# A two-layer hybrid decoder step: the first token rows transposed inside the gate stage instead of ahead of it

## The chip, the cores and the metric

The kernel runs on one core of a Trainium2 chip. A core has five engines, each with its own instruction stream: TensorE (PE in the profile, its weight loads apart as PEld) for matrix products, VectorE (DVE), ScalarE (ACT), GpSimd (POOL) and SyncE (SP), which here only issues loads and stores. ACT and POOL issue loads too. PE writes to PSUM, here five banks for this stage; the other engines take results from there to SBUF, the working memory. The metric is the device time of one execution in microseconds; three runs of the kernel before gave 2650.81, 2652.7 and 2654.59.

## The reference

One inference step over 1,048 token rows of width 1,024: 16 learned meta rows, 1,024 prompt rows, and 8 sample rows that have their own states. Everything is in float32. Layer 0 mixes tokens with a Conformer convolution module, layer 1 with an RWKV-7 recurrence; a squared-ReLU MLP with a hidden width of 4,096 follows each. Only the beginning matters here:

```
def _rmsnorm(x, g):
    y = x * rsqrt(mean(x * x, -1) + RMS_EPS)
    return y * g

hn = _rmsnorm(h, norm_mix[0])
u = hn @ w_pw1 + b_pw1                      # 1024 -> 2048
u = u[..., :D] * sigmoid(u[..., D:])        # the gate
c = depthwise causal convolution of u, 31 taps, + b_dw
out = silu(layernorm(c)) @ w_pw2 + b_pw2
h = h + out
h = h + relu(rmsnorm(h) @ w_in)**2 @ w_out
```

The weights are stored by rows of channels; the vectors (`norm_mix`, `b_pw1` and so on) are small.

## The kernel before, in words

Layer 0 keeps activations with channels on the 128 partitions and tokens along the row, so the 1,024 channels are 8 blocks (`KT`), and the tokens are cut in three groups of 352, 348 and 348 (`G0`). A product in near-float32 precision is made of three (`mm3`, L188): weights and activations are each split into a high part in a shorter format and the low remainder, and high x high, low x high and high x low are added in PSUM. `dense` (L197) does that over the 8 channel blocks, 24 PE products for one block of output channels. The weights' high part is cast by ACT (L158), the low part made by POOL in four pieces (L165); raw weights come by loads on SP into a pool of five buffers tagged "raw".

The input comes with tokens on the partitions. `transpose_x` (L475) turns a group round, in these steps:

1. For group 0, `stage_vecs` (L454) clears a tile on POOL and loads the first small vectors into its rows, every other one by ACT's queue and by POOL's.
2. `load_x` (L436) loads the group's rows in three tiles on SP; for each, ACT squares it with a row sum (L444), takes the root (L445), and DVE the reciprocal (L446).
3. For each channel block, PE transposes the three tiles with the identity into a bank, `tx` (L483), and DVE (group 0) or ACT (group 1) copies it to `h` (L485), which is needed only for the residual add after the convolution module. Group 2 goes through memory.
4. For group 0, `place_vecs` (L462) transposes the staged vectors and copies them to `pvec`, from which all per-channel scales and biases are read.
5. `between` starts the first weight block; then DVE builds `dg`, the identity scaled by each row's reciprocal root (L496).
6. For each channel block, PE multiplies the tiles by `dg`, which transposes and normalizes in one product, `tn` (L500); ACT scales it by `norm_mix` into the high part `hn_h` (L502), DVE makes the low part `hn_l` (L503).

Group 0 goes through all of this before its gate stage. Then `load_dw` (L467) brings in and transposes the 31 depthwise tap weights (`ptw`, L472). The gate stage is `pw1` (L511): for each of 8 blocks of output channels two `dense` calls, `ps_g` and `ps_a`, a sigmoid on ACT and a combining step on DVE (L521).

The instructions carry priorities in program order, and a planner, which simulates a timeline, fixes each engine's order: where an engine would be idle in that timeline, work from later in the program is brought forward. Two things are by hand. Group 0's `transpose_x` runs under `manual_schedule` for ACT (L701), so that ACT's order there is as written. And the work for the next group is mixed into the gate stage by `filler` (L303): `pw1` calls a function 32 times, in the middle of and behind each `dense`, and each call advances a generator so that its units (each `yield` tells how many) are spread evenly over the 32 calls. For group 1 that is `transpose_x(1)` with 4 units for the loads and 8 + 8 for its blocks.

The x tiles come from a pool of three buffers (`xin`), so group 1's loads wait until group 0's tiles have been read for the last time. The convolution of group 0 (L539, L542) runs on DVE from the moment that its inputs and the tap weights are there.

Of the kernel before, what the change touches and what calls it, by code (L numbers as in the profile page):

```python
# [8 lines left out]
F32 = mybir.dt.float32  # L9
# [7 lines left out]
P = 128  # L17
D = 1024
KT = D // P
# [27 lines left out]
def hybrid_step(tc, x_prompt, x_sample, state_conv, state_shift, state_wkv, meta_tokens,  # L47
# [8 lines left out]
    nc = tc.nc  # L56
    ctx = ExitStack()
    with ctx:
# [4 lines left out]
        ident = consts.tile([P, P], F32, name="ident")  # L63
# [9 lines left out]
        d_x2 = dram.tile([P, KT, G0[2][1]], F32, name="d_x2")  # L73
# [32 lines left out]
        col, nrow = {}, 0  # L106
        for name, ap in vecs:
            n = ap.shape[0]
# [85 lines left out]
        def bank(name, tag="mm"):  # L194
            return cur[tag].tile([P, 512], F32, name=name, tag=tag)
# [20 lines left out]
        def tt(name, tag):  # L216
            return cur["tmp"].tile([P, cur["n"]], F32, name=name, tag=tag)
# [178 lines left out]
        with ExitStack() as l0:  # L396
# [16 lines left out]
            h = {}  # L413
# [36 lines left out]
            def load_vecs(tiles):  # L450
                for i in tiles:
                    place_vecs(i, stage_vecs(i))

            def stage_vecs(i):  # L454
                st = cur["raw"].tile([P, D], F32, name=f"stg{i}", tag="raw")[:, :P]
                nc.gpsimd.memset(st, 0.0)
                for q, (name, ap) in enumerate(v for v in vecs if col[v[0]] // P == i):
                    r = col[name] % P
                    (nc.gpsimd if q % 2 else nc.scalar).dma_start(st[r:r + ap.shape[0], :], ap)
                return st  # L460

            def place_vecs(i, st):  # L462
                pt = bank("ptp")
                nc.tensor.transpose(pt[:, :P], st, ident)
                nc.vector.tensor_copy(pvec[:, i * P:(i + 1) * P], pt[:, :P])

            def load_dw():  # L467
                wst = cur["raw"].tile([P, D], F32, name="wst", tag="raw")[:CW, :]
                nc.scalar.dma_start(wst, conv_w_dw.rearrange("l w c -> (l w) c"))
                pt = bank("ptw")  # L470
                for k in range(KT):
                    nc.tensor.transpose(pt[:, k * CW:(k + 1) * CW], wst[:, k * P:(k + 1) * P], ident[:CW, :CW])  # L472
                nc.vector.tensor_copy(wdw, pt[:, :KT * CW].rearrange("p (k w) -> p k w", k=KT))

            def transpose_x(g, ah, al, between=lambda: None):  # L475
                n = G0[g][1]
                staged = stage_vecs(0) if g == 0 else None
                tiles = load_x(xin, g)
                yield 4
                for k in range(KT):  # L480
                    ps = bank(f"tx{g}_{k}")
                    for c, w, xt, ss in tiles:
                        nc.tensor.transpose(ps[:, c:c + w], xt[:w, k * P:(k + 1) * P], ident[:w, :w])  # L483
                    if g < 2:
                        (nc.scalar.copy if g else nc.vector.tensor_copy)(h[g][:, k, :n], ps[:, :n])  # L485
                    else:
                        t = tt(f"xs{k}", "t1")
                        nc.scalar.copy(t[:, :n], ps[:, :n])
                        nc.sync.dma_start(d_x2[:, k, :], t[:, :n])
                    yield 1  # L490
                if g == 0:
                    place_vecs(0, staged)
                between()
                dg = stat(f"dg{g}", "acc0", 1)
                for c, w, xt, ss in tiles:
                    nc.vector.tensor_scalar(dg[:w, c:c + w], ident[:w, :w], ss[:w, 2:3], None, op0=ALU.mult)  # L496
                for k in range(KT):
                    ps = bank(f"tn{g}_{k}")
                    for c, w, xt, ss in tiles:
                        nc.tensor.matmul(ps[:, c:c + w], xt[:w, k * P:(k + 1) * P], dg[:w, c:c + w], start=True, stop=True)  # L500
                    gk = vec("norm_mix", k)
                    nc.scalar.activation(ah[:, k, :n], ps[:, :n], AF.Copy, scale=gk)  # L502
                    nc.vector.scalar_tensor_tensor(al[:, k, :n], ps[:, :n], gk, ah[:, k, :n].bitcast(F32),  # L503
                                                   op0=ALU.mult, op1=ALU.subtract)
                    yield 1

            def pw1_weights(g, m):
                yield load_col(conv_w_pw1[0], KT + m, f"pg{g}_{m}", nc.gpsimd)
                yield load_col(conv_w_pw1[0], m, f"pa{g}_{m}", nc.gpsimd)
# [181 lines left out]
            with ExitStack() as s:  # L691
                TX = 32
                EARLY = 1
                xin = pool(s, "xin", 3)
                fill, rest = filler(8 * KT, ([ranked(CV0, conv(0)), ranked(CV0, ln_silu(0))], EARLY * (15 * KT // 2 + 2 + 2 * MW + KT)))
                for g in range(2):
                    h[g] = residp[(g + 1) % 2].tile([P, KT, N0], F32, name=f"h0_{g}", tag="h")
                acts = [new_act(actp[(g + 1) % 2], f"hn{g}", N0) for g in range(2)]
                ready = []
                first = pw1_weights(0, 0)  # L700
                with tc.manual_schedule(engines={nc.scalar.engine}):  # L701
                    for _ in transpose_x(0, *acts[0], lambda: ready.append(next(first))):
                        pass
                    ready.append(next(first))
                load_dw()
                for g in range(3):
                    nxt, tail = iter(()), ()
                    if g < 2:
                        if g:
                            acts.append(new_act(actp[1], "hn2", N0))  # L710
                        nxt, tail = filler(TX, ([transpose_x(g + 1, *acts[g + 1])], 4 + 2 * KT))

                    def both():
                        if g:
                            fill()
                        if g < 2:
                            nxt()
                    pw1(g, acts[g], both, [] if g else ready)
                    for _ in tail:
                        pass  # L720
                    if g == 0:
                        load_vecs(range(1, ntile))

                zt = xin.tile([P, D], F32, name="zt", tag="xt")[:, :KT * HS].rearrange("p (k t) -> p k t", k=KT)
                nc.gpsimd.memset(zt, 0.0)
                for q in range(4):
                    nc.scalar.dma_start(d_ab[0].rearrange("p k i (j t) -> p k (i j) t", j=2)[:, :, q, :], zt)
                nc.scalar.dma_start(d_v[META:HS, 0:KT * HS], zt[:HS - META].rearrange("p k t -> p (k t)"))
                nc.scalar.dma_start(d_v[META:HS, KT * HS:], zt[:HS - META].rearrange("p k t -> p (k t)"))

                own, prev = (xin.tile([P, D], F32, name=f"lr{s_}", tag="xt").rearrange("p (k c) -> p k c", k=KT) for s_ in "op")
                for cs, j, src in ((HALF[0], 1, rwkv_w1[0]), (HALF[1], 4, rwkv_a1[0])):
                    nc.sync.dma_start(own[:, :, cs], src.rearrange("(k p) c -> p k c", p=P))
                    for k in range(KT):
                        nc.scalar.activation(prev[:, k, cs], own[:, k, cs], AF.Copy, scale=vec("x_mix", j * KT + k))
                for k in range(0, KT, 2):
                    nc.gpsimd.tensor_sub(own[:, k:k + 2], own[:, k:k + 2], prev[:, k:k + 2])
                for s_, t in enumerate((own, prev)):
                    nc.sync.dma_start(d_lr[:, :, s_], t)
# [15 lines left out]
        for i, op in enumerate((ALU.is_gt, ALU.is_ge)):  # L755
            v = m_ar[:HS, i * HS:(i + 1) * HS]
# [448 lines left out]
        st = {"done": -1, "inv": -1, "credit": 0.0, "decoded": False, "free": 0, "normed": -1}  # L1205
# [582 lines left out]
```

## Time and profile before

The execution that was profiled took 2651.75 us; the others are listed above.

| | |
|---|---|
| median of three runs | 2652.7 us |
| profiled execution, whole | 2651.75 us |
| its span, first to last instruction | 2649.8 us |
| PE busy | 2594.1 us, 98% |
| DVE, ACT, POOL busy | 1717.6, 1128.8, 1456.7 us |
| first row transpose on PE | 5.42 us |
| first scaled product (`tn`) | 12.06 us |
| first gate product (`ps_g`) | 20.34 us |
| end of group 0's gate stage on PE | 90 us |

All times within the execution are microseconds from the start of the span. In lists of instructions each line gives start, duration, engine, line of the kernel, operation, tiles, and in brackets how long the engine was idle before and what released it. "q" behind an engine's name is its queue of loads. In the chain of the work that ended last, each line gives start and duration of a piece, followed back from the end at each step to what released it. A product of full float32 operands shows as two records, a transpose as one.

### The profile page before, as it was taken

Reading aid. Unit: us, or ns where it says so; the run is one execution under the profiler, and the core shown is the slowest. Engines: PE = TensorE matmul, PEld = TensorE weight load, DVE = VectorE, ACT = ScalarE, POOL = GpSimd, SP = SyncE. Lnnn points to the kernel's source line nnn. Section 1 sums busy time; section 2 is a strip of 40 time slices with the busy share of each in tenths; the row PEclk is TensorE's granted clock in tenths of the full one; section 3 lists DMA queues with packets and bytes.
Section 4 is the critical chain, followed back from the end, with each engine's and each line's share of the span. In section 5 each row is a group of like instructions: output and inputs, shape, how many; then the busy total and the mean of one; then the engine's idle time right before and its main releaser. Section 6 shows DMA issues by size and latency. Waiting matters only on the chain.

```text
span 2649.8 us, 51719 instructions
## 1 busy us (share of the span) xinstructions
PE 2594.1 (98%) x19956; PEld 2432.9 (92%) x19956; DVE 1717.6 (65%) x3610; ACT 1128.8 (43%) x2093; POOL 1456.7 (55%) x2060
## 2 busy tenths in 40 slices
PE   9999999999999999999999999899999999999998
PEld 8999999999999999777777777789999999999998
DVE  6999999997444444445757567686679554444435
ACT  5546435444444333243344545545444542222223
POOL 7677878878878777022211113476588763333331
PEclk9999999999999999999999999999999999999999
DMA  7663544554446543677776867898575542222211
GB/s 190 172 168 108 167 141 133 160 172 137 138 138 187 155 136 112 191 211 202 214 184 181 213 160 194 218 207 195 142 219 174 153 132 65 72 68 69 72 48 44
DMA packets 602060, 400.24 MB, mean 151 GB/s; under 512 B 96128, under 2 KB 548928, under 8 KB 601814
## 3 DMA queue, kind: packets, MB, share of 16 engines
q1 hardware_dynamic: 573764, 360.08, 49.6%
q0 software_dynamic: 8720, 26.35, 3.0%
q10 hardware_dynamic: 19330, 10.49, 1.4%
q8 instruction: 158, 2.59, 0.4%
q14 instruction: 88, 0.72, 0.1%
HBM read 338.94 MB, written 58.83 MB: 150 GB/s over the span
## 4 chain that ended last, share of the span: by engine, by line
PE 85%; DVE 8%; ACT 2%; issue 2%; DMA 1%; POOL 1%; SPq 0%; ACTq 0%; DVEq 0%; POOLq 0%
PE ps_in L190 8%; PE ps_in L192 8%; PE ps_in L191 8%; PE out L190 8%; PE out L191 8%; PE out L192 8%; PE pk L922 4%; PE pr L922 4%; PE pv L922 3%; PE ps_g L190 1%; PE ps_o L192 1%; PE ps_g L191 1%; PE ps_g L192 1%; PE ps_oo L190 1%; PE ps_o L190 1%
## 5 line engine op out<-in xcount | busy, mean ns | idle before, releaser
L165 POOL TENSOR_TENSOR wo_lo<-wo_raw,wo_hi 128x256 fp32r<-128x256 f32 x736 | 543.0, 770 | 286.6 <-ACT wo_hi L158 279.2
L165 POOL TENSOR_TENSOR wi_lo<-wi_raw,wi_hi 128x256 fp32r<-128x256 f32 x640 | 474.5, 774 | 238.3 <-ACT wi_hi L158 237.9
L190 PE MATMUL out<-hh,wo_hi 128*128 128x352 f32 (+2 forms) x1536 | 497.5, 324 | 8.1 <-DVE h L360 6.5
L360 DVE TENSOR_TENSOR h<-h,out 128x352 f32<-128x352 f32 (+2 forms) x768 | 386.9, 512 | 168.2 <-PE out L192 166.6
L190 PE MATMUL ps_in<-m_h,wi_hi 128*128 128x352 f32 (+2 forms) x1536 | 494.0, 322 | 0.0
L192 PE MATMUL ps_in<-m_l,wi_hi 128*128 128x352 f32 (+2 forms) x1536 | 492.8, 321 | 0.7 <-DVE m_l L288 0.7
L191 PE MATMUL out<-hh,wo_lo 128*128 128x352 f32 (+2 forms) x1536 | 492.5, 321 | 0.0
L191 PE MATMUL ps_in<-m_h,wi_lo 128*128 128x352 f32 (+2 forms) x1536 | 491.5, 320 | 0.0
L192 PE MATMUL out<-hl,wo_hi 128*128 128x352 f32 (+2 forms) x1536 | 490.8, 320 | 0.0
L542 DVE SCALAR_TENSOR_TENSOR cv<-u,wdw,cv 128x348 f32<-128x348 f32 (+2 forms) x720 | 378.8, 577 | 0.7
L158 ACT CAST wi_hi<-wi_raw 128x1024 fp32r<-128x1024 f32 x160 | 167.6, 1049 | 383.7 <-PE out L192 191.1
L158 ACT CAST wo_hi<-wo_raw 128x1024 fp32r<-128x1024 f32 x184 | 192.7, 1048 | 313.0 <-PE out L192 167.1
L190 PEld LDWEIGHTS out<-hh,wo_hi 128*128 128x128 f32 x1536 | 289.1, 188 | 13.7 <-DVE h L360 9.0
L190 PEld LDWEIGHTS ps_in<-m_h,wi_hi 128*128 128x128 f32 x1536 | 289.2, 188 | 1.4
L192 PEld LDWEIGHTS ps_in<-m_l,wi_hi 128*128 128x128 f32 x1536 | 288.2, 188 | 2.0 <-DVE m_l L288 1.5
L191 PEld LDWEIGHTS out<-hh,wo_lo 128*128 128x128 f32 x1536 | 288.5, 188 | 0.8
L191 PEld LDWEIGHTS ps_in<-m_h,wi_lo 128*128 128x128 f32 x1536 | 288.5, 188 | 0.6
L192 PEld LDWEIGHTS out<-hl,wo_hi 128*128 128x128 f32 x1536 | 288.3, 188 | 0.0
L347 DVE SCALAR_TENSOR_TENSOR ps_in<-ps_in,rs_m 128x352 f32<-128x352 f32 (+2 forms) x192 | 100.7, 525 | 256.5 <-PE ps_in L192 256.1
L142 DVE TENSOR_TENSOR hl<-ps_in,hh 128x352 fp32r<-128x352 f32 (+2 forms) x192 | 98.9, 515 | 124.0 <-ACT hh L141 123.9
L1097 POOL DMA_DIRECT2D d_n<-n x32 | 24.5, 764 | 220.4 <-DVE n L1087 130.8
L348 ACT ACTIVATE ps_in<-ps_in 128x352 f32<-128x352 f32 (+2 forms) x192 | 85.1, 444 | 129.4 <-DVE ps_in L347 129.2
(371 smaller groups left out, 4734.5 us busy)
## 6 DMA issues: line engine op xcount, KB each, us to landing
wi_raw<-in_w_mlp_in_dram SPq DMA_DIRECT2D x160, 512.0 KB
wo_raw<-in_w_mlp_out_dram SPq DMA_DIRECT2D x160, 512.0 KB
wk_raw<-in_rwkv_w_k_dram SPq DMA_DIRECT2D x32, 512.0 KB
wr_raw<-in_rwkv_w_r_dram SPq DMA_DIRECT2D x32, 512.0 KB
wv_raw<-in_rwkv_w_v_dram SPq DMA_DIRECT2D x32, 512.0 KB
d_ab<-ab POOLq DMA_DIRECT2D x32, 512.0 KB, 4.3
pg_raw<-in_conv_w_pw_dram SPq DMA_DIRECT2D x24, 512.0 KB
pa_raw<-in_conv_w_pw_dram SPq DMA_DIRECT2D x24, 512.0 KB
```

The source lines that it names most:

```text
L142: return eng_lo.tensor_sub(lo, src, hi.bitcast(F32))
L158: cast = nc.scalar.copy(hi[:, :a * b], raw[:, :a * b])
L165: eng_lo.tensor_sub(lo[:, cs], raw[:, cs], hi[:, cs].bitcast(F32))
L190: nc.tensor.matmul(ps, w[0], act[0], start=first, stop=False)
L191: nc.tensor.matmul(ps, w[1], act[0], start=False, stop=False)
L192: nc.tensor.matmul(ps, w[0], act[1], start=False, stop=last)
L347: nc.vector.scalar_tensor_tensor(s, s, 0.0, rs()[:, :n], op0=ALU.max, op1=ALU.mult)
L348: nc.scalar.activation(s, s, AF.Square)
L360: total = nc.vector.tensor_add(hv[:, 4 * i + m, :], hv[:, 4 * i + m, :], ps[:, :n])
L542: nc.vector.scalar_tensor_tensor(acc[m][:, :n], ug[:, m, j:j + n], wdw[:, m, j:j + 1], acc[m][:, :n], op0=ALU.mult, op1=ALU.add)
L922: nc.tensor.matmul(ps[:, :n], w[:, k, :], act[k], start=k == 0, stop=k == KT - 1)
L1097: nc.gpsimd.dma_start(d_n[ch0:ch0 + ncg, p].rearrange("c r t -> r c t"), n32[:, :ncg])
```

## The change

Five things are done together, all ahead of or inside group 0's gate stage.

- Step 3 for group 0 is no longer done ahead of `between`. It becomes a generator, `rows_in`, and is put on a list, `put_off`. The gate stage's filler runs that list first and then `transpose_x(1)`, so its 32 calls now spread 30 units instead of 20.
- The 16 rows of `norm_mix`, which step 6 needs, get a tile of their own (`nst`) without clearing, loaded first on ACT's queue. `place_norm` transposes them behind the first `tn` block. The other vectors are staged as before, in the remaining rows.
- `place_vecs(0)` for those others, and the transposes of the tap weights, now `place_dw`, become `rest_in`, the first two units of the filler.
- The load of the tap weights moves up: `stage_dw` issues it on ACT's queue ahead of the x tiles, within the order written by hand.
- 16 products of the identity with itself, into a bank that nobody reads, stand ahead of everything on PE.

```
-                for q, (name, ap) in enumerate(v for v in vecs if col[v[0]] // P == i):
+                for q, (name, ap) in enumerate(v for v in vecs if col[v[0]] // P == i and v[0] != "norm_mix"):
...
             def place_vecs(i, st):
                 pt = bank("ptp")
+                own = 0 if i else NM
                 nc.tensor.transpose(pt[:, :P], st, ident)
-                nc.vector.tensor_copy(pvec[:, i * P:(i + 1) * P], pt[:, :P])
-
-            def load_dw():
+                nc.vector.tensor_copy(pvec[:, i * P + own:(i + 1) * P], pt[:, own:P])
+            NM = norm_mix.shape[0] * KT
+
+            def place_norm(st):
+                pt = bank("ptn")
+                nc.tensor.transpose(pt[:, :NM], st, ident[:NM, :NM])
+                nc.vector.tensor_copy(pvec[:, :NM], pt[:, :NM])
+
+            def stage_dw():
                 wst = cur["raw"].tile([P, D], F32, name="wst", tag="raw")[:CW, :]
                 nc.scalar.dma_start(wst, conv_w_dw.rearrange("l w c -> (l w) c"))
+                return wst
+
+            def place_dw(wst):
                 pt = bank("ptw")
...
                 n = G0[g][1]
-                staged = stage_vecs(0) if g == 0 else None
+                if g == 0:
+                    nst = xin.tile([P, P], F32, name="nst", tag="nst", bufs=1)[:NM]
+                    nc.scalar.dma_start(nst, vecs[0][1])
+                    staged, wst = stage_vecs(0), stage_dw()
                 tiles = load_x(xin, g)
                 yield 4
...
+                def rows_in():
+                    for k in range(KT):
+                        ps = bank(f"tx{g}_{k}")
+                        for c, w, xt, ss in tiles:
+                            nc.tensor.transpose(ps[:, c:c + w], xt[:w, k * P:(k + 1) * P], ident[:w, :w])
+                        if g < 2:
+                            (nc.scalar.copy if g else nc.vector.tensor_copy)(h[g][:, k, :n], ps[:, :n])
...
+                        yield 1
+
+                def rest_in():
+                    place_vecs(0, staged)
                     yield 1
-                if g == 0:
-                    place_vecs(0, staged)
+                    place_dw(wst)
+                    yield 1
+                if g:
+                    yield from rows_in()
+                else:
+                    put_off.append(rest_in())
+                    put_off.append(rows_in())
                 between()
...
+                    if g == 0 and k == 0:
+                        place_norm(nst)
                     gk = vec("norm_mix", k)
...
-                ready = []
+                ready, put_off = [], []
                 first = pw1_weights(0, 0)
+                spin = bank("spin")
+                for _ in range(16):
+                    nc.tensor.matmul(spin[:, :P], ident, ident, start=True, stop=True)
...
-                load_dw()
...
-                        nxt, tail = filler(TX, ([transpose_x(g + 1, *acts[g + 1])], 4 + 2 * KT))
+                        nxt, tail = filler(TX, ([*put_off, transpose_x(g + 1, *acts[g + 1])], 4 + 2 * KT + (KT + 2) * bool(put_off)))
+                        put_off.clear()
```

More of the change, by code (lines that the diff above doesn't have):

```diff
@@ L476, in transpose_x @@
                 n = G0[g][1]
-                staged = stage_vecs(0) if g == 0 else None
+                if g == 0:
+                    nst = xin.tile([P, P], F32, name="nst", tag="nst", bufs=1)[:NM]
+                    nc.scalar.dma_start(nst, vecs[0][1])
+                    staged, wst = stage_vecs(0), stage_dw()
                 tiles = load_x(xin, g)
                 yield 4
[L480 to L489, printed above, removed]
-                    yield 1
-                if g == 0:
-                    place_vecs(0, staged)
+                def rows_in():
[6 more added lines that the diff above has]
+                        else:
+                            t = tt(f"xs{k}", "t1")
+                            nc.scalar.copy(t[:, :n], ps[:, :n])
+                            nc.sync.dma_start(d_x2[:, k, :], t[:, :n])
+                        yield 1
+                def rest_in():
+                    place_vecs(0, staged)
+                    yield 1
+                    place_dw(wst)
+                    yield 1
+                if g:
+                    yield from rows_in()
+                else:
+                    put_off.append(rest_in())
+                    put_off.append(rows_in())
                 between()
```

## The prediction

> **What bounds the kernel now.** I read the page's first part, then the waits of PE, then a table of stretches, and last the chain of the first 20 us. The page:
>
> ```profile
> span 2649.8 us, 51719 instructions
> PE 2594.1 (98%) x19956; PEld 2432.9 (92%) x19956; DVE 1717.6 (65%) x3610; ACT 1128.8 (43%) x2093; POOL 1456.7 (55%) x2060
> ```
>
> PE is busy for all but 55.7 us of the span. What it waits for, over the whole run (total, times, longest):
>
> ```profile
> PE pb L814 <- ACT vv L1135: 10.1, 8, 3.6
> PE out L190 <- DVE h L360: 6.5, 7, 1.6
> PE tx L483 <- DMA xt<-in_x_prompt_dram: 5.7, 2, 5.4
> ```
>
> The third row is the start, the only place that the change touches. By stretch (each engine's busy time; the last three columns are granted clock, DMA share, GB/s):
>
> ```profile
> 5.40:20.34 14.94, 13.86 (x81) 12.12 (x81) 8.57 (x22) 8.95 (x19) 2.77 (x4) 1.00 0.85 214
> 20.34:90.20 69.86, 69.86 (x461) 69.65 (x460) 58.63 (x121) 38.60 (x58) 56.16 (x87) 1.00 0.58 163
> ```
>
> From 20.34 to 90.20, the gate stage of the first token group, PE has no gap: an instruction put there costs its full PE time. So only 20.34 us can be shortened, and work taken out of them into the gate stage is paid for again. The chain through them:
>
> ```profile
> 2.18 6.09 DMA xt<-in_x_prompt_dram
> ...
> 8.77 1.82 DVE h L485 x4
> ...
> 11.57 0.35 DVE dg L496
> ...
> 12.06 4.24 PE tn L500 x22
> ...
> 16.32 0.56 ACT hn_h L502
> ...
> 17.55 2.25 PE tn L500 x18
> 19.80 0.61 PE ptw L472 x8
> 20.41 0.36 PE ps_g L190
> ```
>
> The last x tile lands at 8.27. Then come the copies of the transposed rows, which DVE does ahead of the scale matrix dg; then the scaled products tn, the split into hn_h and hn_l, the transposes of the depthwise weights (ptw), and the first gate product at 20.41.
>
> **The pace of PE.** Three groups of instructions (count, busy us, mean ns) and a line of the chain: the first row transposes (5.40 to 8.20), the scaled products of 12.0 to 14.9, and those of group 1 at 64.3 to 65.2.
>
> ```profile
> L483 PE MATMUL tx<-ident,xt 128*128 128x128 f32 x10 | 2.6, 429 | 5.4 <-DMA xt<-in_x_prompt_dram 5.4
> ...
> L500 PE MATMUL tn<-dg,xt 128*128 128x128 f32 x13 | 3.1, 431 | 0.4 <-DVE dg L496 0.4
> ...
> L500 PE MATMUL tn<-dg,xt 128*128 128x128 f32 x4 | 0.6, 274 | 0.0
> ...
> 64.39 0.64 PE tn L500 x6
> ```
>
> The granted-clock column reads 1.00 throughout, so the pace must be read off durations: 13 records in 2.85 us are 0.219 us apart at first, later six fill 0.64 us (the last line, from the chain), 0.107 apart. PE starts at about half pace, and nearly six microseconds of transposes do not lift it; some 3 us of products (12.06 to about 15.0) do. The Trainium skill, "TensorE: Matmul & The Clock Gate", Parts 1 and 4, says the same: about 3.4 us of sustained work opens the gate, an idle window as long closes it, and transposes do not count as work. Here the trace agrees on the opening (2.9 us) and on the transposes; no row shows a closing.
>
> **The change, part by part.**
>
> *Sixteen identity products.* They need only the identity, which POOL has ready at 1.73 us, and PE is idle until 5.42.
>
> ```profile
> 1.44 0.29 POOL masks.py:199 TENSOR_SCALAR_AFFINE_SELECT ident<-ident 128x128 f32<-128x128 f32 x1
> ...
> 11.10 2.77 POOL L165 TENSOR_TENSOR pg_lo<-pg_raw,pg_hi 128x256 fp32r<-128x256 f32 x4 [7.16 <-ACT pg_hi L158]
> ...
> 11.71 0.37 SPq L147 DMA_DIRECT2D pa_raw<-in_conv_w_pw_dram  x1
> ```
>
> (The second and third line are used below.) Each is two records: 32 x 0.219 = 7.0 us if slow throughout, or 2.85 + 19 x 0.107 = 4.9 us if the pace rises as it did for tn. They end between 6.6 and 8.7 us, before or about when the first scale matrix can exist, so they cost 0 to 0.9 us; I take 0.
>
> *Row transposes, their DVE copies, the vector and depthwise transposes leave the front.* What then sets the front is ACT's statistics:
>
> ```profile
> 2.97 0.28 ACTq L459 DMA_DIRECT2D stg<-in_conv_b_pw_dram  x1
> 5.49 0.28 ACTq L459 DMA_DIRECT2D stg<-in_rwkv_a_dram  x1
> 5.81 1.06 ACT L444 ACTIVATE xj<-xt 128x1024 bf16<-128x1024 f32 x1 [3.50 <-DMA stg<-in_norm_mix_dram]
> 6.69 0.23 ACTq L469 DMA_DIRECT2D wst<-in_conv_w_dw_dram  x1
> ...
> 9.73 0.29 ACT L445 ACTIVATE ss<-ss,eps_t 96x1 f32<-96x1 f32 x1
> 9.97 1.05 ACT L158 CAST pg_hi<-pg_raw 128x1024 fp32r<-128x1024 f32 x1
> ...
> 13.40 0.14 DVE L446 RECIPROCAL ss<-ss 96x1 f32<-96x1 f32 x1
> 13.58 0.36 DVE L496 TENSOR_SCALAR dg<-ident,ss 96x96 f32<-96x96 f32 x1
> ```
>
> ACT's queue issued four small loads, then held the fifth until 5.49 and the sixth (wst, behind the first square) until 6.69: each waited for an earlier load to land. After the change all six (nst, four vectors, wst) stand ahead of the first square in ACT's written order. If the sixth is held to 6.69 again, the squares start at 6.95 instead of 5.81; if the earlier issue frees it, they start at 5.81. From there as now: 4.21 us to the end of the third root (5.81 to 10.02), 0.54 for reciprocal and dg (13.40 to 13.94). So dg is whole at 10.6 (early) or 11.7 (late). The products of the first two tiles are done by then, in the gaps. The third tile's first product takes about 0.4 (two records 0.107 apart, the last 0.27 long); the cast of pg (1.05, right behind the root on ACT) ends at 11.05 or 12.2. First hn_h: 11.05 or 12.2, against 16.32.
>
> From hn_h to the gate product it is now 4.09 us with the 0.61 of ptw. Afterwards ptw is gone, but the identity products and the norm transpose take two turns of the five PSUM banks, so four rather than three of the eight tn blocks come behind the first freed bank: 1.2 (16.32 to 17.55) + 4 x 0.64 = 3.8 us. First gate product: 14.9 or 16.0, against 20.41, an advance of 5.5 or 4.4 us. The weights keep up: pg_lo takes 2.8 us behind its cast, so 13.9 or 15.0, and is used column block by column block.
>
> *The same work in the gate stage.* Its price is in the chain at 46.9, where group 1's transposes already run as fillers:
>
> ```profile
> 46.92 0.30 PE tx L483 x3
> 47.22 0.19 PE ps_g L190
> 47.41 0.17 PE ps_g L191
> 47.58 0.17 PE ps_g L192
> ```
>
> That is 0.30 plus 0.04 by which the next two products are longer than 0.16: 0.34 a block, 8 x 0.34 = 2.7 us. ptw brings back its 0.61; the vector transpose about 0.2 (a third of a block and its switch). Returned: 3.5 us. Net: 2.0 (early) or 0.9 (late), middle 1.45.
>
> *What the planner may hoist.* Only ACT's order is written out there; elsewhere a planner fills idle slots with ready work from later in the program:
>
> ```profile
> 19.41 0.82 SPq L441 DMA_DIRECT2D xt<-in_x_prompt_dram  x2
> ...
> 24.07 1.06 ACT L444 ACTIVATE xj<-xt 128x1024 bf16<-128x1024 f32 x1
> ...
> 26.68 0.38 PE L483 MATMUL tx<-ident,xt 128*128 128x128 f32 x2
> ```
>
> The first of group 1's transposes ran at 26.68, though by its share of the filler (7 of 32 calls, each 12 products 0.16 apart, 1.94 us) it was due near 34. After the change PE has gaps between 7 and 12 us with x tiles landed. Hoisted blocks do not come back in the gate stage: between 0 and 2.7 us. I take 0.7 (two blocks), since the one row showing it shows part of one block.
>
> *DVE.* The eight copies (1.82 for four, so 3.7 us) move to about 19 to 38 us. Cover:
>
> ```profile
> DVE ss L446 <- ACT ss L445: 10.9, 2, 7.4
> ...
> 33.33 0.63 DVE L539 TENSOR_SCALAR cv<-u,wdw,pvec 128x352 f32<-128x352 f32 x1
> ```
>
> DVE waits 10.9 us there and starts the convolution only at 33.33. Without that cover, the convolution would start 3.7 us late on an engine that is nearly full afterwards; but its first input comes 4 us earlier. I cost it at 0.
>
> *SP and POOL.* POOL issues four vector loads as before. The staging tiles hold two of five raw buffers until the first two filler calls, so the second pa load slips from 11.7 to about 18 us; its product is due some 12 us after the gate stage starts, at 27. SP's loads of group 1 wait until the last row transpose lets the x tiles go: call 10 of 32, about 16 + 10 x 1.94 + 3.5 = 38.9 us instead of 19.41. The first use is due five calls later, 9.7 us, against 7.3 us today without a wait. Cost 0, bounded below.
>
> **Sum.** 1.45 + 0.7 = 2.1 us gained at the front, nothing elsewhere. The profiled execution took 2651.75 us (span 2649.8 plus 1.95 around it), 1 us under the median of 2652.7; so 2649.6 by that execution, and **2650.6 us** on the median's scale. A measurement here can tell about 0.2% (5.3 us) from no change: this is no measurable change.
>
> **Rivals.**
>
> *The slow pace stays or returns.* Place: tn and the first gate products. If the statistics run late, PE has only scraps from about 7 to 12 us. The price, if it is slow when the hn chain starts: half of 2.9 us, 1.5, or at most 24 records x 0.112 = 2.7 us; the front's gain is gone and the time is 2652 to 2653.3, slower than before by up to 0.6. It decides once more than 2.1 us are lost. Against it: the gap behind the identity products is 0 to 2.5 us. The row on tn has only an opening, so it leaves this case open at 2653; by the Trainium skill's rule (same page, Part 1) a gap under 3.4 us leaves the gate open, and the sum stays at 2650.6. No run here shows that yet.
>
> *Group 1's rows come late.* Place: SP's load at 38.9, with first use at 48.6. Every microsecond of landing beyond 9.7 stalls PE as long, since it takes its queue in order. It is slower than before beyond 11.8 us and beyond 0.2% from 17.1 us: 2658 or more. For it: the load now stands behind fillers and before weight loads on SP. Against: at 19.41 the same load had its first square running 4.7 us later.
>
> *The best front.* Early statistics and all blocks hoisted: 2.0 + 2.7 = 4.7 us, 2648.0. Against: PSUM has five banks, and tn wants them in the same gaps.
>
> *The planner's later order.* It plans layer 0's other engines by a simulated clock; a shift at the start can reorder ties. The waits that could go or double are those of PE on h: 6.5 us in seven. That is 2644 or 2657.
>
> **How the numbers follow.** Forecast (0.9 to 3.4 us gained): 0.50. Slow pace: 0.14. Best front: 0.12. Planner: 0.16, half each way. Late rows: 0.08, five eighths of it beyond 0.2%. Faster by over 0.2%: the planner's better half 0.08 and 0.04 of the best front with help from it, 0.12. Slower: 0.08 + 0.05 = 0.13. Within: 0.75. For 8 in 10 the range leaves out the planner's ends and the late rows: 2646 to 2656; the forecast's own is 2649.3 to 2651.8.
>
> **What would show it.** Right: identity products from about 1.8 us; first hn_h between 11 and 12.5; first ps_g between 14.5 and 16.5; tn records about 0.11 apart there; no PE wait on xt in the first 60 us; the first gate stage longer by 1 to 3.5 us. Wrong: tn records still 0.22 apart, a PE wait on xt near 48, PE gaps in the gate stage, or other waits on h.

## The result, and the profile after

The changed kernel takes 2660.3 us (median of 9 runs), against 2655.0 us for the kernel before on the same chip (9 runs): a ratio of 1.0022, with a 95% interval of 1.0013 to 1.0031. It is slower by 0.22%, 5 to 6 us, where the prediction had 2 us faster and a range that ended at 2656. The profiled execution of the changed kernel took 2660.3 us. These are the first two lines of its page:

```profile
span 2658.5 us, 51785 instructions
...
PE 2598.7 (98%) x19989; PEld 2438.1 (92%) x19989; DVE 1718.6 (65%) x3611; ACT 1129.0 (42%) x2093; POOL 1455.0 (55%) x2060
```

PE is busy 4.6 us longer than before, and its gaps have grown from 55.7 to 59.8 us. The chain of the work that ended last, over the first 25 us of the changed kernel, shows where:

```profile
1.42 3.56 DMA stg<-in_norm_mlp_dram
5.00 10.66 DMA pg_raw<-in_conv_w_pw_dram
15.69 1.04 ACT pg_hi L158
16.73 0.46 ACT hn_h L528
17.22 0.59 DVE hn_l L529
...
17.86 4.16 PE tn L524 x18
22.02 0.35 PE ps_g L190
22.37 0.29 PE ps_g L191
...
23.73 0.16 PE ps_g L190
```

The statistics are no longer in it. What sets the front is `pg`, the load of the first gate weight block: its issue on SP waited until 5.00 for a small load to land (before, it was issued at 2.64), it landed at 15.66, and ACT's written order has the cast of `pg` ahead of the first `hn_h`. PE ran out of work meanwhile. Its waits in the changed kernel (total, times, longest), and then a table of stretches (busy time of PE, PEld, DVE, ACT and POOL, then granted clock, DMA share, GB/s):

```profile
PE out L190 <- DVE h L360: 7.6, 7, 2.3
PE tn L524 <- DVE hn_l L529: 6.1, 1, 6.1
...
PE tx L498 <- DMA xt<-in_x_prompt_dram: 0.9, 1, 0.9
```

```profile
2.00:7.50 5.50, 5.50 (x31) 5.50 (x32) 0.45 (x2) 3.02 (x6) 1.93 (x4) 1.00 0.97 280
...
11.70:17.86 6.16, 0.02 (x1) 0.00 (x1) 0.64 (x2) 2.17 (x4) 1.04 (x2) 0.62 0.35 101
17.86:22.00 4.14, 4.14 (x19) 4.14 (x20) 3.08 (x6) 2.22 (x5) 1.74 (x3) 0.50 0.27 67
22.00:23.60 1.60, 1.60 (x8) 1.60 (x7) 0.58 (x1) 1.54 (x3) 0.00 (x0) 0.54 0.53 160
```

The second line is the hole: PE does 0.02 us of work in 6.16 us. In the third line the granted clock is 0.50, so the eighteen pieces of `tn` behind the hole take 4.16 us, and the first gate products still follow each other at 0.29 instead of 0.16 us. One line of the DMA view (0 to 20 us in 40 slices of half a microsecond) shows what `pg` waited for:

```profile
GB/s 0 0 0 123 140 115 300 366 334 319 394 373 282 218 244 281 270 228 322 306 296 167 35 28 18 105 209 330 326 121 20 19 19 19 20 19 15 0 0 0
```

From 15 to 18.5 us 19 to 20 GB/s flow, where over 300 flowed shortly before: one DMA engine works off what is left of `pg`, and then of a weight load behind it, while the other fifteen are done. The trace's completion records say the same of `pg` alone: of the sixteen that make up its landing, fifteen came between 9.34 and 10.06 us and the last at 15.67.

To see where the difference stays, the starts of the first PE product of some stages are compared (us):

| | before | after | difference |
|---|---|---|---|
| first gate product | 20.34 | 21.73 | +1.39 |
| length of group 0's gate stage, start to start of group 1's | 69.60 | 75.61 | +6.01 |
| end of layer 0's gate stages | 226.20 | 233.02 | +6.82 |
| start of layer 1's mixer | 1075.02 | 1081.89 | +6.87 |

It arises in the first 100 us (1.39 and 6.01, of which 0.58 is won back in the stages of groups 1 and 2) and is then carried unchanged through the next 800. Behind 1075 us the traces of this study differ by several more microseconds in either direction; no run here ties that to the change. The granted clock there is at half for 27.3 us in the kernel before, and the stretch takes 1574.8 us; in the run with the identity products alone (below) it is 10.2 and 1568.2. So the readings go by the table's stages, and the whole times by their intervals.

### The profile page after: what moved, and what is told of

The parts are those of the page before. It is cut to its first block, busy times and chain, and to the rows that moved or that the text cites. A ratio compares the mean times of both kernels' runs of the same rounds, so it can differ in the third digit from the quotient of the medians.

```text
span 2658.5 us, 51785 instructions
## 1 busy us (share of the span) xinstructions
PE 2598.7 (98%) x19989; PEld 2438.1 (92%) x19989; DVE 1718.6 (65%) x3611; ACT 1129.0 (42%) x2093; POOL 1455.0 (55%) x2060
## 4 chain that ended last, share of the span: by engine, by line
PE 83%; DVE 8%; DMA 3%; ACT 2%; issue 1%; POOL 1%; ACTq 0%; SPq 0%; DVEq 0%; POOLq 0%
PE ps_in L190 8%; PE out L190 8%; PE ps_in L192 8%; PE ps_in L191 8%; PE out L191 8%; PE out L192 8%; PE pk L951 4%; PE pr L951 4%; PE pv L951 3%; PE ps_o L192 1%; PE ps_oo L190 1%; PE ps_o L190 1%; PE ps_o L191 1%; PE ps_oo L191 1%; PE ps_oo L192 1%
## 5 line engine op out<-in xcount | busy, mean ns | idle before, releaser
L568 DVE SCALAR_TENSOR_TENSOR cv<-u,wdw,cv 128x352 f32<-128x352 f32 (+2 forms) x720 | 379.5, 577 | 0.6
```

Source lines behind the costliest of these rows:

```text
L568: nc.vector.scalar_tensor_tensor(acc[m][:, :n], ug[:, m, j:j + n], wdw[:, m, j:j + 1], acc[m][:, :n], op0=ALU.mult, op1=ALU.add)
```

## The experiments

Theory A: the early load of the tap rows (`wst`) makes `pg` late, and the slow pace behind the hole follows from that. It has two forms. A1: `wst` and `pg` share a DMA engine. A2: the early issue holds `pg`'s own issue back. The rivals: that the identity products do harm or are useless, and that the work put into the gate stage is what costs. In all of them the time is compared with runs of the kernel before on the same chip.

**The tap rows loaded late.** The load stands behind the first square on ACT again; all else is as in the changed kernel.

```
-                    staged, wst = stage_vecs(0), stage_dw()
+                    staged = stage_vecs(0)
...
-                    place_dw(wst)
+                    place_dw(stage_dw())
```

> The changed kernel with one part undone: the depthwise weights' load (wst) is issued again behind the first square on ACT, not ahead of it; all else stays. Theory A (the first gate weight block pg comes late because its load is held until the seven small loads ahead of it free a slot, and because wst's 31 rows share its path): pg's load is issued by about 3.6 us instead of 5.00, its cast starts by 10.5 instead of 15.69, first hn_h between 11 and 12.5, first gate product between 14.8 and 16.5 instead of 21.73, the granted clock stays at 1.00 once open; the end of layer 0 comes 6 to 8 us earlier than in the changed kernel, so the time is within 2 us of the kernel before (ratio 0.999 to 1.001). Rival B (the loss is the moved work itself, paid for in the gate stage and in waits behind it): the front shortens but the time stays at the changed kernel's ratio of 1.002.

Measured: 2651.69 us against 2654.69, ratio 0.9987 (0.9978 to 0.9995). One moved load turns the loss into a small gain. Its chain:

```profile
0.81 2.30 DMA xt<-in_meta_tokens_dram
3.13 7.15 DMA pg_raw<-in_conv_w_pw_dram
10.30 1.04 ACT pg_hi L158
11.34 0.52 ACT hn_h L528
...
12.52 2.25 PE tn L524 x18
14.77 0.19 PE ps_g L190
```

`pg` is issued at 3.13 behind another, quicker load, lands at 10.28, and the eighteen pieces of `tn` take 2.25 us. The first gate product starts at 14.55, 5.79 us earlier than before. Two rows of the stretches of this kernel, the front and then group 0's gate stage:

```profile
7.50:14.55 7.05, 6.68 (x56) 6.37 (x56) 3.72 (x11) 6.20 (x14) 2.79 (x4) 1.00 0.91 218
14.55:89.39 74.84, 73.94 (x494) 72.78 (x492) 63.18 (x132) 39.94 (x59) 56.12 (x87) 1.00 0.60 167
```

The gate stage is 5.24 us longer than before's 69.60, of which 0.9 is the gap (74.84 less 73.94): PE waits for group 1's x rows. So 5.79 are gained, 5.24 paid back, and by the end of layer 0's gate stages (225.08) the balance is 1.12 us.

**The tap rows in short pieces.** The rows go to a tile with a gap after each 128 columns, so that the load is 248 pieces of 512 bytes; its place is the early one.

```
-                wst = cur["raw"].tile([P, D], F32, name="wst", tag="raw")[:CW, :]
-                nc.scalar.dma_start(wst, conv_w_dw.rearrange("l w c -> (l w) c"))
+                wst = xin.tile([P, KT, P + 2], F32, name="wst", tag="wst", bufs=1)[:CW, :, :P]
+                nc.scalar.dma_start(wst, conv_w_dw.rearrange("l w (a b) -> (l w) a b", b=P))
...
```

> The changed kernel with wst loaded at the same place into rows with a gap behind every 128 columns, so that the load is cut into 248 pieces of 512 bytes instead of 31 rows of 4096. Theory A1 (31 rows go through one of the 16 DMA engines, one after the other for 6 us, and pg's share on that engine queues with them): wst's pieces no longer stand in one line from 7 to 14 us, pg lands by about 11.5, and the time is within 2 us of the first experiment's. Theory A2 (only the moment of issue counts): if pg's load is issued at 5.00 again it lands near 15.7 again and the time stays at 1.002; if it is issued early, this run cannot separate the two.

Measured: 2658.76 us against 2654.69, ratio 1.0016 (1.0007 to 1.0026). The edit did not do what it was made for. The pieces still ran one behind the other, some twenty a microsecond from 11 to 22 us. And in this kernel `pg` went out at 3.13, ahead of the tap rows (5.36), and landed in time, so A1 and A2 are not parted; why the two changed places was not followed. It shows another thing: the tap rows themselves then come too late.

```profile
5.36 17.71 DMA wst<-in_conv_w_dw_dram
...
23.21 0.60 PE ptw L482 x4
23.81 0.59 PE ps_g L192
```

**Without the identity products.** The changed kernel without the 16 products in front.

```
-                spin = bank("spin")
-                for _ in range(16):
-                    nc.tensor.matmul(spin[:, :P], ident, ident, start=True, stop=True)
```

> The changed kernel without the 16 identity products. Theory A: the chain waits for pg until 15.7 whatever PE did before, and the clock is at half when it goes on, as in the changed kernel; time equal to the changed kernel's within 2 us (ratio to before 1.0015 to 1.003). Rival C (the identity products are what costs, by delaying PE or by the clock falling behind them): the time falls by 2 us or more against the changed kernel. Rival D (they help although the clock falls again): slower by 1 to 3 us.

Measured: 2659.16 us against 2654.69, ratio 1.0018 (1.0009 to 1.0027), as the changed kernel. `pg` is issued at 5.10 and cast at 16.17, the clock falls back in the same hole, and the first gate product comes at 22.20. The identity products neither cause the loss nor help here: what they open is closed again before it is used.

**Products in the hole.** The changed kernel with 28 more products, whose result nobody reads, behind the fifth `tn` block; they only keep PE at work until `hn_h` comes.

```
+                    if g == 0 and k == 4:
+                        hold = bank("hold", "x")
+                        for _ in range(28):
+                            nc.tensor.matmul(hold[:, :P], dg[:, :P], ident, start=True, stop=True)
```

> The changed kernel with 28 more products of the scale matrix with the identity, most of them standing behind the fifth scaled block, where PE waits from 11.7 to 17.86; they change nothing but PE's idleness. If the half clock from 13.24 to 23.48 is due to that wait: the granted clock stays 1.00, the 18 records of the last three blocks take under 3 us instead of 4.16, the first gate products are 0.16 apart instead of 0.29, and the time falls by 1.5 to 3 us against the changed kernel (ratio to before about 1.001). If it is not: the same spacing and the same time as the changed kernel.

Measured: 2658.06 us against 2654.69, ratio 1.0014 (1.0005 to 1.0023). `pg` is nearly as late (cast at 15.45 instead of 15.69), but the pace behind it is whole (the chain, and the stretch of the hole with its granted clock of 1.00):

```profile
17.62 2.25 PE tn L524 x18
19.87 0.19 PE ps_g L190
```

```profile
11.70:17.60 5.90, 5.84 (x53) 5.64 (x51) 0.62 (x2) 2.15 (x4) 1.02 (x2) 1.00 0.39 107
```

Layer 0's gate stages end at 230.32, 2.7 us earlier than in the changed kernel. Of these, 0.24 is `pg`'s own, and some 2.5 are the price of the closed gate, 1.9 in `tn` (4.16 less 2.25) and the rest in the gate products. Of the 7.94 us between the changed kernel and the one with the late tap rows (233.02 less 225.08), the other 5.5 are `pg`'s lateness itself (15.66 less 10.28 is 5.4).

**pg held, the tap rows out of the way.** One more small load, which nobody reads, stands ahead of `pg` on SP and holds its issue; the tap rows are loaded only behind the `hn` chain.

```
...
+                if g == 0:
+                    more = xin.tile([P, P], F32, name="more", tag="more", bufs=1)[:8]
+                    nc.sync.dma_start(more, vecs[3][1])
                 between()
...
+                    late_dw.append(stage_dw())
                 for g in range(3):
```

> A look at the trace, to part two reasons for pg's late landing. The first gate weight load is held to about 5 us as in the changed kernel (one more small load on SP's queue takes the slot ahead of it), but wst is loaded only behind the whole hn chain on ACT, so nothing of it is in flight before. Theory A1 (pg's share on one DMA engine waits behind wst's rows): pg issued at about 5.0, lands by 11.5. Theory A2 (the late issue itself): lands near 15.7, 10.7 us after its issue, as in the changed kernel. The taps' transposes then make PE wait for wst in the first gate block, some 5 to 9 us, so the total says nothing here.

Measured, in one execution: 2658.84 us against 2652.31. The total says nothing on the question, because the tap rows now come far too late (PE waits 5.8 us for them). What was asked is in the chain:

```profile
5.44 5.53 DMA pg_raw<-in_conv_w_pw_dram
...
10.99 1.04 ACT pg_hi L158
...
15.56 9.58 DMA wst<-in_conv_w_dw_dram
```

Issued even later than in the changed kernel, `pg` takes 5.53 us instead of 10.66. The hold alone costs less than a microsecond of landing (10.97 against 10.28); it is the company of the tap rows that costs. A2 falls as the main cause. That the rows' way through one engine is what costs, and not their bytes, is left to the next experiment.

**The tap rows in two loads.** The changed kernel, early place and all, with the load cut into 16 rows and 15.

```
-                nc.scalar.dma_start(wst, conv_w_dw.rearrange("l w c -> (l w) c"))
+                taps = conv_w_dw.rearrange("l w c -> (l w) c")
+                nc.scalar.dma_start(wst[:16], taps[:16])
+                nc.scalar.dma_start(wst[16:], taps[16:])
```

> The changed kernel, with the load of the 31 tap rows in two pieces, 16 rows and 15 rows; nothing else is altered, and the early place of the load is kept. Theory A1 (the tap rows are served one behind the other by one DMA engine, and the first gate block's load pg, which has a sixteenth of its bytes on that engine, waits for them there): two loads of 16 and 15 rows go over 16 and 15 engines, both are whole within about 2 us of their issue (by 9 us, against 13.9), and pg, still issued near 5.0 because the load in front of it still holds it, lands near 11, as it did in the run where it was held with the tap rows out of the way (10.97, against 15.66). First hn_h near 12.2, first gate product near 15.7, gate stages of layer 0 end near 226.5, time about 2653, ratio to the kernel before 0.999 to 1.001. Rival A2 (the early issue as such, one more load in a slot, is what costs): pg lands at 15 or later again, first gate product at 21 or later, time about 2660. Slot rival: seven loads ahead instead of six hold pg's issue to 6 or later; then pg lands that much later than 11.

Measured: 2651.86 us against 2653.5, ratio 0.9992 (0.9983 to 1.0001). The loss is gone, by a cut in one transfer: the kernel is level with the one before. The chain and the DMA line of this kernel:

```profile
1.43 3.56 DMA stg<-in_norm_mlp_dram
5.00 6.56 DMA pg_raw<-in_conv_w_pw_dram
11.59 1.04 ACT pg_hi L158
...
13.76 2.25 PE tn L526 x18
16.01 0.19 PE ps_g L190
```

```profile
GB/s 0 0 0 115 123 139 238 345 301 280 377 382 280 247 251 194 138 225 247 283 281 204 282 290 292 290 291 244 44 3 0 0 0 85 202 339 327 129 7 105
```

The hold to 5.00 is the same to the hundredth; `pg` lands 4.1 us earlier, its sixteen completions all between 10.30 and 11.56 us, and the stretch of 19 GB/s is gone. The same bytes are loaded from the same place in the program, so A1 is shown. Tap rows that began in each microsecond, from the packet records of both traces:

| us | 7 | 8 | 9 | 10 | 11 | 12 | 13 |
|---|---|---|---|---|---|---|---|
| one load of 31 rows (changed kernel) | 4 | 5 | 4 | 4 | 5 | 5 | 4 |
| loads of 16 and 15 rows | 16 | 0 | 6 | 9 | 0 | 0 | 0 |

The Trainium skill, "DMA: Bandwidth & Descriptors", section "Why a DMA increments its semaphore by 16 and not by 1", says that a load is spread over the largest number of engines up to 16 that divides its outermost dimension. For 31 rows that is one, for 16 and 15 rows it is 16 and 15. The table agrees, and so do the short pieces above, whose outermost dimension was still 31.

**The late tap rows without identity products.** The kernel of the first experiment without the 16 products.

```
                     staged = stage_vecs(0)
...
-                spin = bank("spin")
-                for _ in range(16):
-                    nc.tensor.matmul(spin[:, :P], ident, ident, start=True, stop=True)
```

> The first experiment's kernel (wst behind the first square) without the 16 identity products: what they are worth once pg is in time. If the clock gate opens only after some 3 us of products: it opens between 11 and 15 us instead of 7.8, the first scaled products are 0.22 apart, the first gate product comes 0.5 to 2.5 us later than at 14.55, ratio to before 0.999 to 1.0. If the products are worth nothing: first gate product within 0.3 us of 14.55 and the same 0.9987.

Measured: 2652.23 us against 2652.31, ratio 0.9997 (0.9988 to 1.0006). Its chain:

```profile
9.37 4.53 PE tn L524 x20
13.92 0.56 ACT hn_h L528
...
15.14 2.25 PE tn L524 x18
17.39 0.19 PE ps_g L190
```

Now the first `tn` blocks are slow, 20 pieces in 4.53 us, and `hn_h` waits for them until 13.92 instead of 11.34; the first gate product starts at 17.17, 2.6 us later. Layer 0's gate stages end 3.1 us later than with the products (228.17 against 225.08). That is 2.0 us later than in the kernel before (226.20), so once `pg` is in time the identity products carry all of the gain.

**The identity products alone.** The kernel before with the 16 products in front and nothing else.

```
+                spin = bank("spin")
+                for _ in range(16):
+                    nc.tensor.matmul(spin[:, :P], ident, ident, start=True, stop=True)
```

> The kernel before, with the 16 identity products in front and nothing else of the change. They run from 1.8 to 7.8 us, as in the changed kernel, so the first row transposes start at about 7.9 instead of 5.42. Theory (PE is opened by products, and what the products are worth is the slow pace of the scaled products behind them): the clock record is full from 6.4 or 7.8 us; if it stays open through the row transposes, the 13 slow products (2.85 us) take half and the first gate product moves from 20.34 to between 19.0 and 20.0, time 0.5 to 1.5 us lower, ratio 0.9995, not to be told from 1. Rival (transposes do not keep the gate open): the clock record is back at half by 13 us, tn records are 0.22 us apart again, and the first gate product comes at 20.3 to 21.5, no gain or a loss of 1 us.

Measured: 2650.92 us against 2653.5, ratio 0.9993 (0.9984 to 1.0002), not to be told from no change. The clock record is full from 6.04 on and stays so, through the row transposes and their waits. The first gate product starts at 20.13, only 0.21 earlier and not by 20.0 as expected, and layer 1's mixer at 1075.16 against 1075.02. The chain of this kernel names what took the gain:

```profile
7.30 12.11 DMA wst<-in_conv_w_dw_dram
...
19.55 0.49 PE ptw L472 x6
```

The load of 31 rows ends at 19.41 and is now the bound of the front. In the kernel before, its last row was through at 17.73 us by the packet records and PE turned to the rows at 19.80, so the load is not on that kernel's chain.

**The row transposes in front again.** The kernel of the first experiment, with the row transposes ahead of `tn`, where they were.

```
-                    put_off.append(rows_in())
                 between()
+                if g == 0:
+                    yield from rows_in()
...
```

> The first experiment's kernel with the row transposes of group 0 back in the front, ahead of the scaled products, as before the change. Theory (PE has the time there, but DVE's copies stand ahead of the last scale matrix): first hn_h between 12 and 14, first gate product between 15.5 and 18; the gate stage is 4 to 5 us shorter than in the first experiment, since the fillers and the wait for group 1's rows are gone; layer 0 ends 0.5 to 3 us earlier than there, ratio to before 0.997 to 0.9985. Rival (putting the rows off is itself the gain): layer 0 ends later than in the first experiment.

Measured: 2654.93 us against 2652.31, ratio 1.0007 (0.9998 to 1.0016): no gain over the whole, where 0.15 to 0.3% was expected. Up to 224.26, the end of layer 0's gate stages, it is 0.8 us ahead of the first experiment: the first gate product comes 2.9 us later (17.47), the gate stage is 3.7 shorter (71.13). Then 3.75 us are lost between 256 and 516 us, in the middle of layer 0's MLPs. One wait of PE there and the stretch around it:

```profile
PE out L190 <- DVE h L360: 2.4, 1, 2.4
```

```profile
438.00:446.00 8.00, 5.62 (x26) 5.33 (x25) 8.00 (x16) 6.24 (x12) 8.00 (x10) 0.79 0.26 74
```

PE waits 2.38 us for DVE, and then the granted clock is at half for 3.4 us (0.79 over the eight). Why DVE is later there was not followed.

**The row transposes among the scaled products.** The same, but the transposes stand behind `tn` in the program and use two PSUM banks of another pool, so that the planner can mix them with `tn`.

```
-                        ps = bank(f"tx{g}_{k}")
+                        ps = bank(f"tx{g}_{k}") if g else psc.tile([P, 512], F32, name=f"tx{g}_{k}", tag="cv")
...
-                    put_off.append(rows_in())
...
+                if g == 0:
+                    yield from rows_in()
...
```

> The first experiment's kernel with group 0's row transposes behind the scaled products in program order and in two PSUM banks of their own (those of the convolution, idle then), so that the planner fits them into PE's gaps between 7.8 and 12.5 us: first gate product between 14.5 and 16.5, gate stage 4 to 5 us shorter than in the first experiment, layer 0 ends 3 to 5 us earlier than there, ratio to before 0.996 to 0.998. If the gaps are not there or DVE's copies delay the low parts: first gate product behind 17 and no gain over the first experiment.

Measured: 2646.51 us against 2652.31, ratio 0.9974 (0.9965 to 0.9983): faster than both kernels. The chain, and the stretches of front and gate stage:

```profile
9.31 1.76 PE tn L523 x14
11.07 0.61 PE tx L498 x6
11.68 1.56 PE tn L523 x14
13.24 0.61 PE tx L498 x6
```

```profile
7.50:16.26 8.76, 7.97 (x73) 7.59 (x70) 6.23 (x17) 6.68 (x14) 2.79 (x4) 1.00 0.83 203
16.26:86.57 70.31, 70.31 (x470) 69.86 (x468) 59.42 (x123) 39.74 (x58) 56.07 (x87) 1.00 0.61 173
```

The front is 1.71 us longer than with the transposes as fillers, and the gate stage 4.53 shorter, because it has neither the eight blocks nor the wait for group 1's rows. A part of the transposes runs where PE had nothing else to do, and all of it at full pace. The new place and the two banks were not tried apart.

## Why the prediction was wrong

The step that failed is in its part on the row transposes: "the cast of pg (1.05, right behind the root on ACT) ends at 11.05 or 12.2". It took for granted that `pg`'s load lands as before. The same assumption stands in "*SP and POOL.* POOL issues four vector loads as before", where a later weight load and group 1's rows were followed and `pg` was not. The prediction asked of the moved load what it does to ACT's squares ("early" or "late"), and not what it does to the other transfers in flight. Measured, the cast ended at 16.73: the load of 31 rows ran on one DMA engine from 7 to 14 us, and the sixteenth of `pg` on that engine came last. There was no reserve to take it: in the kernel before `pg`'s last completion is recorded at 9.95, and the cast that the prediction shows starts at 9.97. In the first experiment `pg` lands at 10.28 (3.13 + 7.15), and even there it is this load that the chain of the front runs through.

The second step that failed is the rival of the slow pace. Its mechanism came true and its size did not: the gap was "0 to 2.5 us" in the prediction and 6.1 us in the trace. The gate closed there, at a cost of some 2.5 us by the run with products in the hole, as against 1.5 or at most 2.7 in the prediction. By the rule it cited, of the Trainium skill, "TensorE: Matmul & The Clock Gate", Part 1, a gap under 3.4 us leaves the gate open. The hole is longer than that, but the clock record fell at 13.24 already, 1.5 us into it, although PE was busy without a gap from 7.50 to 11.70. And in the run with the row transposes in front the clock was at half after a gap of 2.38 us. The kernel before has such a place too, in layer 1, whose rows the prediction, with its "no row shows a closing", did not read: PE waits 2.1 us from 1425.14 on, and soon after it goes on the granted clock is 0.50.

```profile
1428.50:1431.80 3.30, 3.30 (x9) 2.27 (x7) 3.30 (x9) 0.00 (x0) 1.62 (x4) 0.50 0.33 97
```

It is not so each time: a gap of 2.9 us at 1274.59 in the run with the identity products alone left the clock full, and so did one of 1.6 us, the longest wait for `h` in layer 0 of the first experiment. The measurement decides, and a gap of two microseconds is not safe.

The other steps, point by point:

- *Identity products:* right where they can be seen. They run from 1.78 to 7.81 and the clock is full from 6.41; no cost of them shows, and they are worth 3.1 us once `pg` is in time.
- *Early or late statistics:* early, the squares start at 5.21, and in the run with the late tap rows the third root ends at 10.01, as against 10.02. First `hn_h` at 11.34 and first gate product at 14.55 there, against 11.05 and 14.9; the 0.3 in `hn_h` is the wait for `pg`.
- *Returned work:* 3.5 us in the prediction, and the gate stage of the first experiment is 5.24 longer. The price of a row block was right: in that trace seven of the eight are three transposes in one piece and delay the gate products by 0.34 each, as in the two lines below (0.30, and 0.19 instead of 0.16); the eighth is cut in two and costs 0.44. That is 2.8, against 2.7. The two small transposes were mis-sized: 1.1 instead of 0.81, with `ptw` in two halves that each pay for a switch. The wait for group 1's rows costs 1.1, and 0.2 was not followed. Where only the two small transposes come back (the last experiment) the stage is 70.31, 0.7 longer than before.

```profile
24.06 0.30 PE tx L498 x3
24.36 0.19 PE ps_g L190
```

- *Group 1's rows late:* the rival came true at 0.9 us of idleness, 1.1 with the slow start behind it, below the 2.1 from which it would decide.
- *Planner hoisting:* 0 instead of 0.7. The first group 0 row transpose of the changed kernel runs at 27.8 us; none was brought forward.
- *DVE:* 0, as said; no wait of PE in group 0's gate stage is on it.

Put together for the run with the late tap rows: 5.79 gained in front, 5.24 paid back, and 0.57 gained in the stages of groups 1 and 2, which no term foresaw and which was not followed: 1.12. That it lies inside the prediction's 0.9 to 3.4 is luck, since without the 0.57 it is 0.55; the front held, the balance did not. The changed kernel has the same 5.24 and 0.58, with 0.77 on top, most of it slow gate products, and 1.39 lost in front.

## What to carry to other kernels

When a transfer is moved, list every other transfer that is in flight with it, and see how each is spread over the DMA engines: a load of 31 rows, a number without a divisor from 2 to 16, went through one engine here and held up the share of other loads on that engine. Cut such a load into pieces, here 16 rows and 15. And when a step leaves the path, look at how close behind it the next input lands: here `pg` landed just as its cast could begin, and the tap rows some two microseconds ahead of their use, and neither load was on the chain of the kernel before.

## What the runs showed of the hardware

- 31 rows of 4 KB in one load took 6.5 to 6.7 us, one behind the other, about 19 GB/s. A load of 512 KB beside them took 10.66 us, against 6.56 with the rows in two loads and 5.53 with none of them in flight.
- Row transposes from 5.42 us on did not open the clock gate in the kernel before, where the clock record is full only from 15.34, behind the first scaled products. After identity products had opened it, it stayed open through row transposes and short waits from 6.04 us on (the run with the identity products alone).
- The gate closed behind gaps of 2.07 us (the kernel before, layer 1) and 2.38 us (the run with the row transposes in front), and 1.5 us into the hole of the changed kernel; a gap of 2.9 us in the run with the identity products alone left it open.
- The granted-clock column read 1.00 in the cold start both before and after (2.00 to 7.50 above, where 32 records of the identity products took 6.03 us, 0.19 apart, and the clock record itself is full only from 6.41), and 0.50 once the gate had closed. It shows a closing, not a gate that has yet to open.
